# Three of a feed-forward layer's column groups by seven products of quarters: a two-layer fp32 trunk on one core

## The chip, the core and the metric

The kernel runs on one core of a Trainium2 chip. A core has five engines that run side by side, each with its own in-order queue of instructions: PE (TensorE, the matmuls; its weight loads are a second row, PEld), DVE (VectorE), ACT (ScalarE), POOL (GpSimd) and SP (SyncE, which here issues nearly all transfers). Transfers run on 16 DMA engines. Operands lie in SBUF; matmuls write into PSUM, which has eight banks of 128 x 512 fp32 values.

The metric is the device time of one execution in microseconds (us). Of before three runs are shown, and their median counts. One more execution was taken with the hardware profiler, and all durations below come from it.

## The reference

`x` has 256 tokens of width 1024, in fp32. There are two layers (`DEPTH` 2); the feed-forward width `D_FF` is 2816.

```python
def swiglu(h, w_gate, w_up, w_down):
    return (jax.nn.silu(h @ w_gate) * (h @ w_up)) @ w_down

for l in range(DEPTH):
    x = x + 0.5 * swiglu(rms_norm(x, ffn1_norm[l]), ffn1_w_gate[l], ffn1_w_up[l], ffn1_w_down[l])
    proj = rms_norm(x, mix_norm[l]) @ w_in[l]
    ...   # windowed attention out_a and differential attention out_b, from column ranges of proj
    x = x + jnp.concatenate([out_a, out_b], axis=-1) @ w_out[l]
    x = x + 0.5 * swiglu(rms_norm(x, ffn2_norm[l]), ffn2_w_gate[l], ffn2_w_up[l], ffn2_w_down[l])
return rms_norm(x, final_norm)
```

So there are four feed-forward layers (FFN 1 to 4) and two attention mixers, in the order FFN 1, mixer, FFN 2, FFN 3, mixer, FFN 4.

## The kernel before

**Three products for one.** A matmul in the type fp32r takes rounded fp32 operands. Every value v is therefore split in two: hi is v rounded to fp32r (a copy with a cast, on ACT) and lo is v - hi (a subtraction, on DVE, which writes fp32r). A product is the sum of hi x hi, lo x hi and hi x lo: three matmuls into the same PSUM bank (lines 317 to 319, `tokens`).

**The weights come in steps.** A list `specs` holds all weight loads in the order of their use; one step of the FFN is 1 MB: 4 row blocks of 128 by 512 columns. `emit_load(i)` takes the buffers `raw`, `whi` and `wlo` of step i (three of each), issues the transfer on SP's queue, and then, in two halves of 128 x 1024, the cast (ACT, line 106) and the subtraction (DVE, line 108). `weights()` hands out the operands of the step that is used now, and emits the loads of all steps up to `LOOK` = 2 ahead. A step makes 24 matmuls, since it meets both halves of the tokens (t = 0, 1).

**The FFN** (`ffn`). The hidden width is cut in column groups of 512: group 0, groups 1 to 4, and a last half group. The loop of groups 1 to 4:

```python
            hT = turn(h, 2)
            gs, us = [bank(), bank()], [bank(), bank()]
            for sl in (gs, us):
                for k0 in (0, 4):
                    tokens(sl, norm.xs, weights(), k0)
            h = hidden(gs, us)
            for hh in range(2):
                down(hT, g - 1, hh, weights())
```

Group g's gate and up columns take four steps (two row halves `k0` for each), 96 matmuls; `hidden` applies silu (ACT, line 379) and the product with up (DVE, line 384) to the four banks; and the down product of the group before it, two steps and 48 matmuls, covers that. At the head of the next group PE transposes the hidden block (8 transposes, line 398) and `split` makes its operand (lines 323 and 324). The down product adds into four banks that are held through the whole FFN.

**The operands of x.** `Norm.pair(j)` transposes two column blocks of `xk` and writes hi (ACT, line 185, from PSUM with the gain as scale) and lo (DVE, line 186). The norm's factor per token comes later, as the scale of silu and of the up product, so only these operands must be there before an FFN begins. At the end of an FFN or a mixer the residual is added (`Residual.add`, line 366), followed by the squares for the next norm (ACT, line 175); two of the four pairs are made before the last products, and two (`late`) after the next stage has begun.

**The mixers.** Eight steps of w_in and w_out there have the second half of each subtraction on POOL instead of DVE (`pooled`, line 107). The end of a mixer's head norm for the differential heads (lines 619 to 633) comes after all of the products of probabilities and values.

**The start.** SP issues the first two steps' transfers in quarters, alternating with the four transfers of x.

**Who sets the order.** Instructions are written in program order, and the framework's scheduler, which has a timeline model, may reorder them on each engine by priority; a tile pool hands a buffer out again only when its last reader is done.

Of the kernel before, what the change touches and what calls it, by code (L numbers as in the profile page):

```python
# [27 lines left out]
LOOK = 2  # L28
N_RAW, N_HI, N_LO = 3, 3, 3
N_S4 = 18  # L30
# [3 lines left out]
def trunk(ctx: ExitStack, tc: tile.TileContext, x, n1, g1, u1, d1, nm, w_in, sink,  # L34
# [29 lines left out]


    specs = []
    loaded = {}
    paired = set()
    pooled = set()
# [6 lines left out]
    def plain(w, c0, n, k0=0, kn=None):  # L76
        src = rows(w, c0, n, k0, kn)
        kn = src.shape[1]
        return (kn, n, lambda t: [(t, src)])

    def emit_load(i):
        kn, n, moves = specs[i]
        raw = wp.tile([P, kn, n], F32, tag="raw", bufs=N_RAW, name=nm_("raw"))
# [4 lines left out]
        for dst, src in moves(raw):  # L88
            if i > 1:
                sp.dma_start(dst, src)  # L90
            else:
                for a, b in zip(cuts, cuts[1:]):
                    sp.dma_start(dst[:, a:b], src[:, a:b])
                    yield
        for a, b in zip(cuts, cuts[1:]):
# [9 lines left out]
            for r_, h_, l_ in views:  # L105
                act.copy(h_, r_)  # L106
                eng = pool if i in pooled and a in cuts[2:] else dve
                eng.tensor_tensor(l_, r_, f(h_), op=ALU.subtract)  # L108
            if i < 2:
                yield  # L110
    nxt = [0, 0]

    def weights():
        i = nxt[0]
        nxt[0] += 1
        while i > 1 and nxt[1] <= min(i + LOOK, len(specs) - 1):
            for _ in emit_load(nxt[1]):
                pass
            nxt[1] += 1
        return loaded.pop(i)  # L120

    for l in range(DEPTH):
        def ffn_specs(wg, wu, wd):
# [3 lines left out]
            for g in range(1, NGRP):  # L127
                specs.extend(plain(w[l], g * 512, 512, k0, 4) for w in (wg, wu) for k0 in (0, 4))
                specs.extend(down(g - 1, h) for h in range(2))
            for k0 in (0, 4):  # L130
                def gu_moves(t, k0=k0, ws=(wg[l], wu[l])):
                    return [(t[:, :, h * 256:h * 256 + 256], rows(w, FF - 256, 256, k0, 4)) for h, w in enumerate(ws)]
                specs.append((4, 512, gu_moves))
# [10 lines left out]
        for c in range(2):  # L144
            def qa_moves(t, c=c, wi=wi):
                return [(t[:, :, h * P:(h + 1) * P], rows(wi, QA + h * 256 + c * P, P)) for h in range(2)]
            paired.add(len(specs))
            specs.append((KC, 256, qa_moves))
        for k0 in (0, 4):
            specs.append(plain(wi, VB, 512, k0, 4))  # L150
        pooled.update(range(mixed + 4, len(specs)))
# [3 lines left out]
        for k0 in (0, 2):  # L155
# [3 lines left out]
            specs.append((2, D, o_moves))  # L159
# [6 lines left out]
    class Norm:  # L166


        def __init__(self, g0):
            self.g0, self.xs = g0, []  # L170
            self.ss = tmp("nss", 2, (P, 2, 4))

        def squares(self, t, c, n):
            j_ = tmp("junk", 2, (P, 512))
            self.last = act.activation(j_[:, :n], xk[:, t, c:c + n], AF.Square, accum_out=self.ss[:, t, c // 256:c // 256 + 1])

        def pair(self, j):
            sl = halves(bank())
            for i in range(2):
                for t in range(2):  # L180
                    pe.transpose(sl[:, i, t * P:(t + 1) * P], xk[:, t, (2 * j + i) * P:(2 * j + i + 1) * P], ident)
            xs = blk()
            for i in range(2):
                g = gcol[:, self.g0 + 2 * j + i:self.g0 + 2 * j + i + 1]
                act.activation(xs[:, i, 0:S], sl[:, i], AF.Identity, scale=g)  # L185
                dve.scalar_tensor_tensor(xs[:, i, S:512], in0=sl[:, i], scalar=g, in1=f(xs[:, i, 0:S]),  # L186
                                         op0=ALU.mult, op1=ALU.subtract)
            self.xs.append(xs)
# [25 lines left out]
    early = [emit_load(0), emit_load(1)]  # L214
    for j in range(4):
        sp.dma_start(xk[:, :, j * 256:(j + 1) * 256], x[0].rearrange("(t p) d -> p t d", p=P)[:, :, j * 256:(j + 1) * 256])
        for e in early * 2 if j < 2 else ():
            next(e)
    nxt[1] = 2
# [13 lines left out]
    def take_x(k):  # L233

        if k < 2:
            for j in (2 * k, 2 * k + 1):
                norm.pair(j)
                for e in early * 2 if k == 0 else ():
                    next(e)
        else:  # L240
            for t in range(2):
                for h in range(2):
                    norm.squares(t, h * 512, 512)

    grow = const.tile([NG - 16, P], F32, name="grow")
    dist_i = const.tile([P, 512], mybir.dt.int32, name="dist_i")
# [7 lines left out]
    lin = const.tile([P, 4, DEPTH * 64], F32, name="lin")  # L254
    lsum = const.tile([P, 2, DEPTH], F32, name="lsum")
    lpr = const.tile([P, 2, DEPTH * 64], F32, name="lpr")
# [6 lines left out]
    def attention_constants():  # L263
# [6 lines left out]

        pool.iota(dist_i, pattern=[[P, 2], [-1, S]], base=0, channel_multiplier=1)
# [21 lines left out]

        for i, a in enumerate((lq1, lk1, lq2, lk2)):
            pool.dma_start(lin[:, i], a.rearrange("l d -> (l d)").partition_broadcast(P))

    def make_lam():
        for i in range(2):
# [43 lines left out]
    def first_groups(norm, ws):  # L342

        sls = [halves(bank()) for _ in ws]
        for k in range(0, KC, 2):
            if k == 4:
                norm.late()
# [12 lines left out]
    class Residual:  # L360
# [5 lines left out]
        def add(self, h, t):  # L366
            xv = xk[:, t, h * 512:(h + 1) * 512]
            dve.tensor_tensor(xv, xv, self.accs[h][t], op=ALU.add)
            self.nxt.squares(t, h * 512, 512)

        def turn(self, h):
            for j in (2 * h, 2 * h + 1):
                self.nxt.pair(j)

    def ffn(norm, aside=None, before=None, final=False):
        def gate(acc, t):
            g = tmp().rearrange("p a n -> p (a n)")
            n = acc.shape[1]
            act.activation(g[:, :n], acc, AF.Silu, scale=norm.r[:, t:t + 1])  # L379
            return g[:, :n]  # L380

        def up(h, acc, g, t):
            n = acc.shape[1]
            dve.scalar_tensor_tensor(h[:, t, :n], in0=acc, scalar=norm.hr[:, t:t + 1], in1=g, op0=ALU.mult, op1=ALU.mult)  # L384
# [7 lines left out]
        def turn(hs, n):  # L392
            out_ = []
            for i in range(n):
# [5 lines left out]
                split(hb, sl)  # L400
# [10 lines left out]
        for k0 in (0, 4):  # L411
            if before is not None:
                before(k0 // 4)
            elif k0 == 4:
                norm.late()
            ws = (weights(), weights())
            for k in (0, 2):
                for sl, w in zip((gs, us), ws):
                    tokens(sl, norm.xs, w, k0, (k, k + 1))
        if before is not None:  # L420
            before(2)
            norm.stats()
        h = hidden(gs, us)
        for g in range(1, NGRP):
            hT = turn(h, 2)
            gs, us = [bank(), bank()], [bank(), bank()]
            for sl in (gs, us):
                for k0 in (0, 4):
                    tokens(sl, norm.xs, weights(), k0)
# [3 lines left out]
            if g == 2 and aside is not None:  # L433
                with tc.issue_after(norm.last.ins):
                    aside()
# [16 lines left out]
    def ffn_close(parts, nxt):  # L452
# [11 lines left out]
        def late():  # L464
            res.turn(1)
            nxt.stats()
        nxt.late = late

    def mix(l, norm, nxt_norm):
# [15 lines left out]
        def q_finish(sl, sc):  # L485
            t = tmp()
            q = tp.tile([P, 2, 512], F32R, tag="q", bufs=3, name=nm_("q"))
            for i in range(2):
                dve.scalar_tensor_tensor(t[:, i], in0=sl[:, i], scalar=sc[i], in1=norm.R, op0=ALU.mult, op1=ALU.mult)
            split(q, t)  # L490
# [118 lines left out]
        oa = [bank() for _ in range(2)]  # L609
        for t in range(2):  # L610
            for c in range(4):
                for a in range(2):
# [6 lines left out]
        ss = tmp("ss", 1, (P, 2, HB))  # L619
        for h in range(HB):  # L620
            for t in range(2):
                j_ = tmp("junk", 2, (P, P))
                act.activation(j_, osl[t][:, h * P:(h + 1) * P], AF.Square, accum_out=ss[:, t, h:h + 1])
        d1 = den_b.rearrange("p h (t a) -> p a t h", a=2)[:, 0]
        dd = tmp("dd", 1, (P, 2, HB))
        dve.scalar_tensor_tensor(dd, in0=d1, scalar=EPS, in1=d1, op0=ALU.mult, op1=ALU.mult)
        dve.scalar_tensor_tensor(ss, in0=ss, scalar=1.0 / P, in1=dd, op0=ALU.mult, op1=ALU.add)
        rb = tmp("rb", 1, (P, 2, HB))
        pool.tensor_tensor(rb.rearrange("p t h -> p (t h)"), ss.rearrange("p t h -> p (t h)"), mhalf, op=ALU.pow)
        on = blk(F32)  # L630
        for t in range(2):
            dve.tensor_tensor(on[:, t].rearrange("p (h d) -> p h d", h=HB), osl[t].rearrange("p (h d) -> p h d", h=HB),
                              rb[:, t].unsqueeze(2).to_broadcast([P, HB, P]), op=ALU.mult)
# [18 lines left out]
        for hp, src in enumerate(turned(on)):  # L652
            dst = oT[2 + hp]
            act.activation(dst[:, :, 0:S], src, AF.Copy, scale=gsub[:, l:l + 1])
            dve.scalar_tensor_tensor(dst[:, :, S:512], in0=src, scalar=gsub[:, l:l + 1], in1=f(dst[:, :, 0:S]),
# [126 lines left out]
```

## Time and profile before

| quantity | value |
| --- | --- |
| median of three runs | 998.27 us (995.05 to 998.62) |
| the profiled execution | 997.01 us, span 995.2 us |
| mean granted PE clock in it | 0.991 of full speed |
| DMA | 169.39 MB, mean 170 GB/s, 51.3% of 16 engines' time on SP's queue |
| costliest rows, busy time | L317, L318, L319 on PE 433, 439, 437 us; L108 on DVE 375.8; L106 on ACT 323.2 |
| mean of one, 128 x 1024 | L108 1222 ns x256, L106 1050 ns |
| chain of waits, by engine | PE 90%, DVE 3%, ACT 3%, issue 2%, DMA 2% |

The rows of single matmuls overlap (their ends are modelled), so the three rows of PE add to more than its busy time; how long PE takes for one is read from the length of a stretch divided by the matmuls in it. The idle time of an engine has a releaser: what ended last of what the next instruction waited for. Idle time of an engine that doesn't set the end costs nothing. L106's idle time ends with PE's L318, that is, with the matmuls that give a `whi` buffer back: ACT and DVE prepare weights as fast as PE uses them up.

### The profile page before, as it was taken

How to read it: one execution, taken by the hardware profiler on the slowest of the kernel's cores; microseconds unless marked ns; L12 is line 12 of the kernel's file. 1: busy time of each engine (PE TensorE's matmuls, PEld its weight loads, DVE VectorE, ACT ScalarE, POOL GpSimd, SP SyncE). 2: the span in 40 equal slices, each digit the busy share in tenths (PEclk: the TensorE clock that was granted, in tenths of full speed). 3: DMA queues.
4: the chain of work that ended last, by engine and by line, in shares of the span. 5: the costliest groups of instructions: out<-in, count | busy, mean ns of one | idle time of the engine just before them, and what ended most of it. 6: DMA issues, size and time to landing. Idle time of an engine off the chain costs nothing.

```text
span 995.2 us, 12394 instructions
## 1 busy us (share of the span) xinstructions
PE 961.8 (97%) x4940; PEld 813.7 (82%) x4940; DVE 550.0 (55%) x816; ACT 476.7 (48%) x809; POOL 53.6 (5%) x78
## 2 busy tenths in 40 slices
PE   6999999999999999999999999999999999999996
PEld 5788888889798788888878888887988887888885
DVE  4645454568945555454555545456597455454553
ACT  5544443457745443434445343435477355444433
POOL 4000000004100000000000000000230000000001
PEclk9999999999999999999999999999999999999999
DMA  8655565635515555656545565555445245565531
GB/s 264 212 195 186 174 206 173 204 97 182 150 43 169 178 202 172 196 182 200 181 143 194 172 209 170 192 188 184 118 142 152 85 169 169 190 212 187 195 127 42
DMA packets 98218, 169.39 MB, mean 170 GB/s; under 512 B 3182, under 2 KB 30896, under 8 KB 98160
## 3 DMA queue, kind: packets, MB, share of 16 engines
q1 hardware_dynamic: 97872, 168.31, 51.3%
q0 software_dynamic: 288, 0.30, 0.4%
q8 instruction: 38, 0.62, 0.2%
q14 instruction: 20, 0.16, 0.0%
HBM read 167.54 MB, written 1.05 MB: 169 GB/s over the span
## 4 chain that ended last, share of the span: by engine, by line
PE 90%; DVE 3%; ACT 3%; issue 2%; DMA 2%; SPq 0%; POOLq 0%; POOL 0%; ACTq 0%; DVEq 0%
PE ps L317 25%; PE ps L318 25%; PE ps L319 25%; PE ps L398 2%; PE ps L338 2%; PE ps L339 2%; PE ps L340 2%; DMA raw<-in_ffn_w_up_dram 2%; PE ps L615 1%; DVE wlo L108 1%; ACT whi L106 1%; PE ps L567 1%; PE ps L502 1%; ACT s L512 1%; PE ps L588 1%
## 5 line engine op out<-in xcount | busy, mean ns | idle before, releaser
L108 DVE TENSOR_TENSOR wlo<-raw,whi 128x1024 fp32r<-128x1024 f32 (+2 forms) x364 | 375.8, 1076 | 338.0 <-ACT whi L106 336.1
L106 ACT CAST whi<-raw 128x1024 fp32r<-128x1024 f32 (+2 forms) x392 | 323.2, 882 | 356.0 <-PE ps L318 322.4
L317 PE MATMUL ps<-whi,s 128*128 128x512 f32 x1126 | 433.2, 393 | 6.2 <-ACT s L185 5.3
L318 PE MATMUL ps<-whi,s 128*128 128x512 f32 x1126 | 439.0, 390 | 0.0
L319 PE MATMUL ps<-wlo,s 128*128 128x512 f32 x1126 | 437.0, 390 | 0.0
L317 PEld LDWEIGHTS ps<-whi,s 128*128 128x128 f32 x1126 | 211.8, 189 | 49.7 <-ACT s L185 5.8
L318 PEld LDWEIGHTS ps<-whi,s 128*128 128x128 f32 x1126 | 212.6, 189 | 43.8 <-DVE s L186 0.5
L319 PEld LDWEIGHTS ps<-wlo,s 128*128 128x128 f32 x1126 | 212.3, 189 | 43.5
L338 PE MATMUL ps<-s,whi 128*128 128x256 f32 x224 | 64.8, 293 | 4.3 <-ACT s L185 4.3
L339 PE MATMUL ps<-s,whi 128*128 128x256 f32 x224 | 64.9, 290 | 0.0
L340 PE MATMUL ps<-s,wlo 128*128 128x256 f32 x224 | 64.4, 288 | 0.0
L379 ACT ACTIVATE tmp<-ps,r 128x512 f32<-128x512 f32 (+1 forms) x48 | 31.2, 651 | 62.9 <-PE ps L319 62.8
L384 DVE SCALAR_TENSOR_TENSOR s<-ps,hr,tmp 128x512 f32<-128x512 f32 (+1 forms) x48 | 32.7, 705 | 41.2 <-PE ps L319 24.7
L338 PEld LDWEIGHTS ps<-s,whi 128*128 128x128 f32 x224 | 43.5, 196 | 5.6 <-ACT s L185 4.8
L339 PEld LDWEIGHTS ps<-s,whi 128*128 128x128 f32 x224 | 44.3, 198 | 0.1
L340 PEld LDWEIGHTS ps<-s,wlo 128*128 128x128 f32 x224 | 44.3, 198 | 0.0
L196 POOL TENSOR_TENSOR r<-ms,mhalf 128x2 f32<-128x2 f32 x6 | 4.2, 706 | 637.7 <-DVE ms L194 637.7
L512 ACT ACTIVATE s<-s,negm 128x256 f32<-128x256 f32 x64 | 31.8, 499 | 12.4 <-DVE negm L510 12.3
L324 DVE TENSOR_TENSOR s<-ps,s 128x512 fp32r<-128x512 f32 x48 | 31.0, 684 | 8.2 <-ACT s L323 8.2
L108 POOL TENSOR_TENSOR wlo<-raw,whi 128x256 fp32r<-128x256 f32 (+1 forms) x28 | 31.7, 1156 | 62.4 <-ACT whi L106 62.4
L323 ACT CAST s<-ps 128x512 fp32r<-128x512 f32 x48 | 25.7, 583 | 12.1 <-PE ps L398 9.7
L398 PE MATMUL ps<-ident,s 128*128 128x128 f32 x176 | 24.7, 274 | 4.3 <-DVE s L384 4.3
(115 smaller groups left out, 456.4 us busy)
## 6 DMA issues: line engine op xcount, KB each, us to landing
raw<-in_ffn_w_down_dram SPq DMA_DIRECT2D x44, 1024.0 KB, 4.9
raw<-in_ffn_w_gate_dram SPq DMA_DIRECT2D x39, 1024.0 KB, 5.0
raw<-in_ffn_w_up_dram SPq DMA_DIRECT2D x39, 1024.0 KB, 5.0
raw<-in_w_in_dram SPq DMA_DIRECT2D x14, 1024.0 KB, 5.1
raw<-in_ffn_w_gate_dram SPq DMA_DIRECT2D x8, 512.0 KB, 3.7
raw<-in_ffn_w_up_dram SPq DMA_DIRECT2D x8, 512.0 KB, 4.7
raw<-in_w_in_dram SPq DMA_DIRECT2D x8, 512.0 KB, 4.6
raw<-in_w_out_dram SPq DMA_DIRECT2D x4, 1024.0 KB, 4.8
```

What stands on the lines that cost most here:

```text
L106: act.copy(h_, r_)
L108: eng.tensor_tensor(l_, r_, f(h_), op=ALU.subtract)
L317: pe.matmul(accs[t], lhsT=xh, rhs=hi[:, k], start=kk == first, stop=False)
L318: pe.matmul(accs[t], lhsT=xl, rhs=hi[:, k], start=False, stop=False)
L319: pe.matmul(accs[t], lhsT=xh, rhs=lo[:, k], start=False, stop=kk == (last if isinstance(last, int) else last[t]))
L338: pe.matmul(acc, lhsT=wh, rhs=xv[:, 0:S], start=first and i == 0 and j == 0, stop=False)
L339: pe.matmul(acc, lhsT=wh, rhs=xv[:, S:512], start=False, stop=False)
L340: pe.matmul(acc, lhsT=wl, rhs=xv[:, 0:S], start=False, stop=last and i == len(kcs) - 1 and j == 1)
L379: act.activation(g[:, :n], acc, AF.Silu, scale=norm.r[:, t:t + 1])
L384: dve.scalar_tensor_tensor(h[:, t, :n], in0=acc, scalar=norm.hr[:, t:t + 1], in1=g, op0=ALU.mult, op1=ALU.mult)
L398: pe.transpose(sl[:, c, t * P:(t + 1) * P], hs[:, t, (2 * i + c) * P:(2 * i + c + 1) * P], ident)
L512: act.activation(e[:, t, c], e[:, t, c], AF.Exp, scale=-1.0, bias=negm[:, n:n + 1], accum_out=den[:, n:n + 1])
```

## The change

In groups 1, 3 and 4 of every FFN (`SEVEN`) the four steps of gate and up are taken as a product of 2 x 2 quarters. On one side stand the quarters of x: tokens in two halves t, rows in two halves b (x00, x01, x10, x11). On the other side stand four weight quarters of 1 MB: a and d of gate (upper and lower rows), b and c of up. The eight products of a quarter by a quarter become seven (Strassen's method in Winograd's form), with sums around them: four sums of x's quarters, made once for each FFN (`make_sums`), four differences of weight quarters for each group, written in place over a raw buffer (`less`), and seven additions of 128 x 512 results for each group (`plus`). A product is now 12 matmuls, and its weight operand is used once.

Around it: six raw buffers in place of three, and transfers up to eight steps ahead, separate from the split (`AHEAD`); operands of x for an FFN go through an fp32 copy in SBUF (`operands`), since the sums need it; POOL's share of the splits goes to DVE; x is loaded on ACT's queue; group 1's transposes come after its first product (before: ahead of it); the residual's squares come after the transposes of x; the second pair of operands and the stats are spread over the next stage's first steps (`late(k)`); the head norm `norm_b` is put ahead of the last 8 of the other heads' 32 products of probabilities and values; and instructions that PE waits for get a higher priority (`urgent`).

```diff
-LOOK = 2
-N_RAW, N_HI, N_LO = 3, 3, 3
-N_S4 = 18
+LOOK, AHEAD = 2, 8
+N_RAW, N_HI, N_LO = 6, 3, 3
+N_S4 = 16
+SEVEN = (1, 3, 4)
...
+    def urgent():
+        return tc.high_priority(300)
...
+    def seven(wg, wu, c0, downs):
+        a, b, c, d = [object() for _ in range(4)]
+        def less(x, y, to):
+            def prep():
+                for h in (0, 2):
+                    x_, y_, t_ = [raws[i][:, h:h + 2] for i in (x, y, to)]
+                    dve.tensor_tensor(t_, x_, y_, op=ALU.subtract)
+            return prep
+        n = dict(kn=4, n=512, moves=None)
+        return [plain(wg, c0, 512, 0, 4, key=a, free=[]),
+                Step(4, 512, plain(wu, c0, 512, 0, 4).moves, key=b, prep=less(b, a, a), src=a, free=[]),
+                Step(4, 512, plain(wu, c0, 512, 4, 4).moves, key=c, prep=less(c, b, b), src=b),
+                Step(**n, prep=less(c, a, a), src=a, free=[]),
+                downs[0],
+                plain(wg, c0, 512, 4, 4, key=d, free=[]),
+                Step(**n, prep=less(d, a, d), src=d, free=[a, d]),
+                Step(**n, src=c),
+                downs[1]]
...
-                eng = pool if i in pooled and a in cuts[2:] else dve
-                eng.tensor_tensor(l_, r_, f(h_), op=ALU.subtract)
+                dve.tensor_tensor(l_, r_, f(h_), op=ALU.subtract)
...
+    at = dict(use=0, dma=2, prep=2, split=2)
     def weights():
-        while i > 1 and nxt[1] <= min(i + LOOK, len(specs) - 1):
-            for _ in emit_load(nxt[1]):
-                pass
-            nxt[1] += 1
+        i = at["use"]
+        at["use"] += 1
+        if i > 1:
+            while True:
+                if at["split"] <= min(i + LOOK, len(specs) - 1) and at["prep"] > at["split"]:
+                    for _ in emit_split(at["split"]):
+                        pass
+                    at["split"] += 1
+                elif at["prep"] <= min(i + LOOK + 1, len(specs) - 1) and at["dma"] > at["prep"] and \
+                        (specs[at["prep"]].prep is None or at["split"] >= at["prep"]):
+                    if specs[at["prep"]].prep is not None:
+                        specs[at["prep"]].prep()
+                    at["prep"] += 1
+                elif at["dma"] < min(i + AHEAD, len(specs)) and (specs[at["dma"]].moves is None or len(raws) < N_RAW):
...
+                    at["dma"] += 1
+                else:
+                    break
...
+        def operands(self, j, sl):
+            if self.sums:
...
+                for i in range(2):
+                    act.activation(xg[:, i], sl[:, i], AF.Identity, scale=g)
+                self.last_act = act.copy(xs[:, :, 0:S], xg)
+                self.last = dve.tensor_tensor(xs[:, :, S:512], xg, f(xs[:, :, 0:S]), op=ALU.subtract)
+                return
...
+        def make_sums(self):
+            (t0, t1), (b0, b1) = [(t[:, :, 0:P], t[:, :, P:S]) for t in self.xg]
+            def make(x, y, op):
+                v = tmp().rearrange("p a (c s) -> p (a c) s", c=2)
+                dve.tensor_tensor(v, x, y, op=op)
+                sm = blk().rearrange("p a (c s) -> p (a c) s", c=2)
+                act.copy(sm[:, :, 0:P], v)
+                dve.tensor_tensor(sm[:, :, P:S], v, f(sm[:, :, 0:P]), op=ALU.subtract)
+                self.sm.append(sm)
+                return v
+            s1 = make(t1, b1, ALU.add)
+            s2 = make(s1, t0, ALU.subtract)
+            make(t0, t1, ALU.subtract)
+            make(b0, s2, ALU.subtract)
...
-        sp.dma_start(xk[:, :, j * 256:(j + 1) * 256], x[0].rearrange("(t p) d -> p t d", p=P)[:, :, j * 256:(j + 1) * 256])
+        act.dma_start(xk[:, :, j * 256:(j + 1) * 256], x[0].rearrange("(t p) d -> p t d", p=P)[:, :, j * 256:(j + 1) * 256])
...
+        def late(self, k):
+            if k == 2:
+                self.turn(1)
+            elif k == 3:
+                self.nxt.stats()
...
+        def by_seven(h, g):
+            flat = lambda: tmp().rearrange("p a n -> p (a n)")
+            if g > 1:
+                hT = turn(h, 2)
+            acc = prod(norm.quarter(0, 0))
+            m1 = flat()
+            with urgent():
+                act.copy(m1, acc)
+            if g == 1:
+                hT = turn(h, 2)
+            m5 = prod(norm.summed(0))
+            m7 = prod(norm.summed(2))
+            m6 = prod(norm.summed(1))
+            u2 = plus(flat(), m1, m6)
+            u3 = plus(flat(), u2, m7)
+            u1 = plus(flat(), u3, m5)
+            plus(u2, u2, m5)
+            down(hT, g - 1, 0, weights())
+            acc = prod(norm.quarter(0, 1))
+            h = blk(F32)
+            g0 = plus(m1, m1, acc)
+            with urgent():
+                act.activation(g0, g0, AF.Silu, scale=norm.r[:, 0:1])
+            acc = prod(norm.quarter(1, 1))
+            g1 = plus(u3, u3, acc)
...
+            up(h, u1, g1, 1)
+            acc = prod(norm.summed(3))
+            plus(u2, u2, acc)
+            up(h, u2, g0, 0)
+            down(hT, g - 1, 1, weights())
+            return h
```

In the built program PE has 4362 instructions in the place of 4510, DVE 851 for 609, ACT 520 for 432, POOL 50 for 61, and SP 177 for 180.

More of the change, by code (lines that the diff above doesn't have):

```diff
@@ L233, in take_x @@
     def take_x(k):
[L235 to L239, printed above, removed]
-        else:
-            for t in range(2):
-                for h in range(2):
-                    norm.squares(t, h * 512, 512)
+        if k < 4:
+            norm.pair(k)
+            for e in early * 2 if k < 2 else ():
+                next(e)
+        else:
+            with tc.issue_after(norm.last_act.ins):
+                for t in range(2):
+                    for h in range(2):
+                        norm.squares(t, h * 512, 512)
+            norm.stats()
     grow = const.tile([NG - 16, P], F32, name="grow")
-    dist_i = const.tile([P, 512], mybir.dt.int32, name="dist_i")
     distB = const.tile([P, 2, S], F32, name="distB")
@@ L399, in turn @@
                 hb = blk()
[L400 removed]
+                with urgent():
+                    split(hb, sl)
                 out_.append(hb)
@@ L410, in ffn @@
         gs, us = [bank(), bank()], [bank(), bank()]
[L411 to L422, printed above, removed]
+        if before is None:
+            before = norm.late
+        before(0)
+        ws = (weights(), weights())
+        for k in (0, 2):
+            before(k // 2 + 1)
+            for sl, w in zip((gs, us), ws):
+                tokens(sl, norm.xs, w, 0, (k, k + 1))
+        before(3)
+        for sl in (gs, us):
+            tokens(sl, norm.xs, weights(), 4)
+        before(4)
         h = hidden(gs, us)
         for g in range(1, NGRP):
[L425 to L429, printed above, removed]
+            if g == 3 and aside is not None:
+                with tc.issue_after(norm.last.ins):
+                    aside()
+            if g in SEVEN:
+                h = by_seven(h, g)
+                continue
+            if g > 1:
+                hT = turn(h, 2)
+            gs = [bank(), bank()]
+            tokens(gs, norm.xs, weights(), 0)
+            if g == 1:
+                hT = turn(h, 2)
+            tokens(gs, norm.xs, weights(), 4)
+            us = [bank(), bank()]
+            for k0 in (0, 4):
+                tokens(us, norm.xs, weights(), k0)
             h = hidden(gs, us)
```

217 lines of the change are left out of this document (134 added, 83 removed).

## The prediction

> **What bounds the kernel now.** I read the page's busy shares first, then the idle gaps of PE along the timeline, then one steady column group in the view by windows and in DVE's timeline.
>
> ```profile
> PE 961.8 (97%) x4940; PEld 813.7 (82%) x4940; DVE 550.0 (55%) x816; ACT 476.7 (48%) x809; POOL 53.6 (5%) x78
> ...
> 404.22:437.75 33.53, 33.53 (x154) 27.86 (x153) 16.80 (x16) 14.15 (x17) 0.00 (x0) 1.00 0.58 188
> ...
> 371.56 2.36 DVE L108 TENSOR_TENSOR wlo<-raw,whi 128x1024 fp32r<-128x1024 f32 x2 [3.07 <-ACT whi L106]
> 373.83 1.28 DVE L324 TENSOR_TENSOR s<-ps,s 128x512 fp32r<-128x512 f32 x2
> ```
>
> The second line is one column group between two turns of the hidden block (start and length; busy time of PE, PEld, DVE, ACT, POOL; clock, DMA). PE never rests there; DVE is half idle, and its idle time ends with ACT's cast, which itself waits for PE to give a buffer back. A group has 144 matmuls (96 gate and up, 48 down) and 8 transposes (0.87 us in the chain): (33.53 - 0.87) / 144 = 0.2268 us a matmul. Its DVE work is six splits of 2.36, two hidden-block splits of 1.28 together and two up products of 1.43 together: 16.9. The third line gives DVE's rate when nothing holds it: two halves of a split take 373.83 - 371.56 = 2.27, so 1.135 each, though one alone lasts 1.222 (row L108, 302.4 us over 256).
>
> PE's real losses are few, and they lie at stage borders:
>
> ```profile
> 206.09 0.50 PE L338 MATMUL ps<-s,whi 128*128 128x256 f32 x2 [2.15 <-ACT s L185]
> 256.15 1.45 PE L502 MATMUL ps<-s,q 64*128 64x256 f32 x20 [2.02 <-DVE q L324]
> 336.86 0.44 PE L398 MATMUL ps<-ident,s 128*128 128x128 f32 x2 [1.58 <-DVE s L384]
> 502.77 1.29 PE L317 MATMUL ps<-whi,s 128*128 128x512 f32 x4 [1.96 <-ACT s L185]
> ...
> 207.00:210.00 3.00, 3.00 (x16) 3.00 (x15) 3.00 (x11) 2.36 (x7) 0.71 (x1) 0.50 0.82 231
> ...
> 311.00:314.00 3.00, 3.00 (x18) 2.55 (x17) 3.00 (x6) 2.44 (x6) 0.00 (x0) 1.00 0.06 16
> ```
>
> In brackets stands the idle time before, and its releaser. After the gap at 206 PE ran at clock 0.50 until 210. The last line is the border from the first mixer to the FFN after it: no PE idle at all.
>
> **The sum's base.** The profiled execution took 997.0 (span 995.2); the median of the runs is 1.3 above it. About 0.5% (5 us) is what a measurement here can tell from no change.
>
> **1. The products removed.** In each of twelve groups (three per FFN) seven products of 12 matmuls replace eight: 12 x 0.2268 = 2.72 a group, 32.7 in all if PE stays the bound. A new group needs 132 x 0.2268 + 0.87 = 30.8 of PE.
>
> **2. What DVE gets in those groups.** Seven weight operands, each used once, replace four used twice: nine splits a group instead of six, so 18 halves; and four quarter differences in place, 8 halves. In the trace no such difference exists; the nearest row is the split's own subtraction, same size, both inputs in SBUF: 1.135 unheld, 1.222 if each waits for the one before. I take 1.135, since in the built program's lists the two halves of a difference read data finished earlier. 26 x 1.135 = 29.5. Seven additions of 128x512 with an input in PSUM (row L324, 0.64): 4.5. With 1.28 and 1.43 as before: 36.7, against PE's 30.8 and the old period of 33.5. ACT gets 18 casts of 1.0, a copy and the rest: 21, no bound. So DVE becomes the bound inside the group, and what helps is only what it does ahead, in the half-idle group before; three hi and lo buffers and a look-ahead of two limit that.
>
> For groups 3 and 4, which follow each other, I went down the built program's queues of PE, ACT and DVE, each instruction starting when its engine, inputs and buffer are free and lasting as above. Group 2 comes out at 33.5, as measured. Groups 3 and 4 need 66.3 together: PE's 61.6, and waits of 0.8 before group 4's transposes, 1.3 at its fourth product, 0.7 at its fifth to seventh, 2.0 before the transposes after it. That last one can be checked by eye: behind the last product's bank DVE has listed an addition, two split halves, an addition, a split half and the up product, 0.64 + 2.27 + 0.64 + 1.14 + 0.7 = 5.4, while PE has 20 down matmuls, 4.5, and ACT's cast for the last half comes late. Before: 67.1. Gain 0.8 of 5.4.
>
> Group 1 of FFNs 2 to 4, from the end of group 0 to the next transposes: 34.8 (waits 0.7, 1.2, 2.2) against 33.5 + 1.58: gain 0.3. So 1.1 an FFN for the three: -3.3; groups 3 and 4 of the first FFN: -0.8.
>
> **3. The entries of FFNs 2 to 4.** Before, ACT writes the rounded operand from PSUM directly (L185, 0.46) and PE starts. Now it writes both halves in plain fp32 to SBUF and then casts them (0.55), with other casts listed between. After the mixer's last matmul ACT's list holds a square (0.62), two operand passes (0.84), two weight casts that wait for the buffer PE has just left (2.0), then the cast: 4.0 before PE's first matmul. The border at 311 cost nothing. At the third FFN: two casts 2.0, square 0.63, four passes 1.7, square 0.63, cast 0.55: 5.5, against 1.96 above. Sum: 4.0 + 3.5 + 4.0 = +11.5. These waits are not in the trace; between zero (if the list lets PE cover them) and this, I take the list.
>
> **4. The clock.** A gap near 2 us brought half clock for 3.4 us (1.7 us lost) at 206, 502 and 694, and not at 255 nor at 336 (1.58). Two entries newly get a gap of 4: +3.4. Six gaps near 2 (four behind group 4, two behind group 1) at half odds: 6 x 0.5 x 1.7 = +5, bounds 0 and 10. The Trainium skill (TensorE: Matmul & The Clock Gate, in the table on what matters for kernels) warns only of gaps above about 3 us; by it the six would cost nothing and the sum would be 5 lower. The trace has half clock after 1.96 and 2.15, so the trace decides.
>
> **5. The start.** x comes on ACT's queue, loads 2 and 3 no longer wait for a raw buffer: at the 259 GB/s of the first 26 us, 5 MB are in by about 22, and group 0 ends near 33 instead of 38. But the first up product stands on DVE behind the difference c - b; c is the eighth MB (2.2 + 8 x 1.05 MB / 0.26 = 34), so the transposes start near 40 as before (39.7), only with 12 matmuls done; and DVE's debt, 6.4 of waiting before group 2, takes that back and 1.9 more. Bounds -5 and +6. One half-clock stretch goes, one comes.
>
> **6. The mixers.** POOL's split halves go to DVE. They cost DVE time already:
>
> ```profile
> 242.52 3.34 DVE L108 TENSOR_TENSOR wlo<-raw,whi 128x512 fp32r<-128x512 f32 x2
> ...
> 242.31 2.99 POOL L108 TENSOR_TENSOR wlo<-raw,whi 128x512 fp32r<-128x512 f32 x2 [5.29 <-ACT whi L106]
> ```
>
> Two that alone take 1.28 took 3.34 beside POOL; four on DVE alone are 2.56. So -1 a mixer (the gap at 255 stands behind the second such pair), and -0.5 for the head norm put between the last products (gap at 288, 0.45): -3. Bounds -6 and +6. The Trainium skill (SBUF, Who interferes with whom) says that a vector instruction with two SBUF inputs and a GpSimd instruction that reads SBUF lock each other out; the trace agrees here. One who counted POOL's work as free help would have added 7 a mixer instead.
>
> **Sum.** -3.3 - 0.8 + 11.5 + 3.4 + 5 + 1.9 - 3 = +14.7; a third of the differences held (1.222) adds 96 x 0.087 / 3 = 2.8. 997.0 + 17.5 = 1014.5.
>
> **The rivals.**
> *PE stays the bound.* DVE runs far enough ahead, groups fall to 30.8, entries are covered as at 311: 997 - 33 = 964; half of it, 981. For: DVE is at 55% and the order was rebuilt with priorities for what PE waits for. Against: 36.7 over 30.8, and only two steps of lead. 0.20, of which 0.07 for the full gain.
> *A draw.* The entries are hidden, the rest stands: 1014.5 - 15 = 1000. 0.10.
> *Every DVE instruction held.* All 26 at 1.222: 12 x 26 x 0.087 = 27 more than 1.135, so 1039; it decides once DVE waits on itself in each chain, for the additions too. The Trainium skill (VectorE: DVE Perf Modes, on the drain) says that the next instruction does not start before the pipe is empty, and that one that isn't held starts earlier; the 2.27 of the pair supports the second half. 0.10.
> *Loads late.* Two of six raw buffers (a and c) are held through most of a group; if SP's in-order queue, where each load waits for a buffer, falls behind by one landing (4.9) in each of the twelve: +59, 1070. Against: DMA is at 58% in a group, and loads are listed several steps ahead. 0.05, and 0.05 for part of it.
> *The forecast*, DVE-bound groups without gain and longer entries: 0.50, alone within 1003 to 1028.
>
> The range 984 to 1036 leaves out the full gain and the upper ends of the last two. Faster 0.20, same 0.10, slower 0.70.
>
> **What would show it.** Right: DVE over 95% busy in groups 3 and 4, near 66 for the pair; PE idle released by DVE before transposes; gaps of 4 to 5.5 released by ACT at three entries; more stretches at clock 0.5. Wrong: periods near 31, PE idle under 1% in them (steps 2 and 3 fall); differences at 1.22 start to start (the drain); PE waiting for raw (the loads).

## The result, and the profile after

The changed kernel took 1000.5 us (median of 12 runs, 998.35 to 1001.19) against 997.35 of the kernel before in the same series: 1.0029 times as long, 95% interval 1.0019 to 1.0038. That is 0.3% slower, inside what the prediction called no change; it had forecast 1014.5. The profiled execution took 999.4, span 997.4.

The page's busy shares and, below them, its chain by engine:

```profile
PE 938.8 (94%) x4796; PEld 788.0 (79%) x4796; DVE 799.9 (80%) x1112; ACT 577.7 (58%) x927; POOL 25.7 (3%) x50
...
PE 77%; DVE 15%; ACT 4%; issue 2%; DMA 1%; POOL 0%; POOLq 0%; DVEq 0%; ACTq 0%
```

PE has 144 instructions and 23 us less, DVE 250 us more, and DVE stands in the chain with 15% in place of 3%. FFN 2 by windows, from the end of group 0: group 1, 2, 3, 4 (columns as before):

```profile
339.47:372.35 32.88, 31.00 (x141) 25.38 (x139) 32.88 (x36) 22.92 (x25) 0.00 (x0) 1.00 0.64 218
372.35:405.96 33.61, 33.61 (x152) 27.93 (x153) 21.76 (x21) 12.26 (x14) 0.00 (x0) 1.00 0.48 162
405.96:437.61 31.65, 30.97 (x141) 25.47 (x139) 31.26 (x34) 20.55 (x23) 0.00 (x0) 1.00 0.58 200
437.61:472.05 34.44, 31.91 (x140) 25.30 (x141) 34.44 (x36) 21.97 (x25) 0.00 (x0) 1.00 0.56 187
```

DVE never rests in groups 1 and 4. Group 2 (eight products) is as long as before, and DVE has 5 us more in it than its own 16.8: that is the work it does ahead for group 3. PE's timeline, the waits that matter:

```profile
73.34 0.69 PE L574 MATMUL ps<-ident,s 128*128 128x128 f32 x2 [6.08 <-DVE s L509]
314.21 2.07 PE L431 MATMUL ps<-whi,s 128*128 128x512 f32 x4 [3.65 <-ACT s L263]
372.35 1.09 PE L574 MATMUL ps<-ident,s 128*128 128x128 f32 x8 [1.88 <-DVE s L509]
472.05 0.44 PE L574 MATMUL ps<-ident,s 128*128 128x128 f32 x2 [1.53 <-DVE s L509]
505.99 2.08 PE L431 MATMUL ps<-whi,s 128*128 128x512 f32 x4 [4.17 <-ACT s L263]
```

Two kinds: an FFN's first matmul waits for ACT's cast of the operand (L263; 802.87 has a third, 3.64), and transposes wait for DVE's up product (L509). ACT's timeline at 311 shows the detour with the weight casts inside it:

```profile
310.92 0.84 ACT L262 ACTIVATE s<-ps,gcol 128x256 f32<-128x256 f32 x2
311.63 2.00 ACT L147 CAST whi<-raw 128x1024 fp32r<-128x1024 f32 x2
313.52 0.64 ACT L263 CAST s<-s 128x512 fp32r<-128x512 f32 x1
```

### The profile page after: what moved, and what is told of

Read it like the earlier page. It is cut to its first block, busy times and chain, and to the rows that moved or that the text cites. A ratio compares the mean times of both kernels' runs of the same rounds, so it can differ in the third digit from the quotient of the medians.

```text
span 997.4 us, 12586 instructions
## 1 busy us (share of the span) xinstructions
PE 938.8 (94%) x4796; PEld 788.0 (79%) x4796; DVE 799.9 (80%) x1112; ACT 577.7 (58%) x927; POOL 25.7 (3%) x50
## 4 chain that ended last, share of the span: by engine, by line
PE 77%; DVE 15%; ACT 4%; issue 2%; DMA 1%; POOL 0%; POOLq 0%; DVEq 0%; ACTq 0%
PE ps L431 15%; PE ps L432 15%; PE ps L433 15%; DVE wlo L148 8%; PE ps L516 5%; PE ps L518 5%; PE ps L517 5%; DVE raw L104 4%; PE ps L452 3%; PE ps L453 3%; PE ps L454 3%; DVE tmp L527 2%; ACT whi L147 2%; PE ps L574 2%; PE ps L832 1%
## 5 line engine op out<-in xcount | busy, mean ns | idle before, releaser
L147 ACT CAST whi<-raw 128x1024 fp32r<-128x1024 f32 (+2 forms) x464 | 396.3, 909 | 288.0 <-PE ps L432 112.0
L148 DVE TENSOR_TENSOR wlo<-raw,whi 128x1024 fp32r<-128x1024 f32 (+2 forms) x464 | 462.9, 1042 | 114.1 <-ACT whi L147 113.2
L431 PE MATMUL ps<-whi,s 128*128 128x512 f32 x742 | 286.4, 396 | 14.2 <-ACT s L263 13.3
L432 PE MATMUL ps<-whi,s 128*128 128x512 f32 x742 | 290.8, 392 | 0.0
L433 PE MATMUL ps<-wlo,s 128*128 128x512 f32 x742 | 283.7, 392 | 0.0
L431 PEld LDWEIGHTS ps<-whi,s 128*128 128x128 f32 x742 | 141.0, 191 | 44.8 <-ACT s L263 14.8
L433 PEld LDWEIGHTS ps<-wlo,s 128*128 128x128 f32 x742 | 140.6, 190 | 30.1 <-DVE wlo L148 1.7
L432 PEld LDWEIGHTS ps<-whi,s 128*128 128x128 f32 x742 | 141.2, 190 | 28.4
L516 PE MATMUL ps<-whi,s 128*128 128x512 f32 x336 | 132.7, 395 | 3.4 <-ACT whi L147 3.4
L517 PE MATMUL ps<-whi,s 128*128 128x512 f32 x336 | 130.9, 389 | 0.0
L518 PE MATMUL ps<-wlo,s 128*128 128x512 f32 x336 | 129.2, 392 | 0.3 <-DVE wlo L148 0.2
L104 DVE TENSOR_TENSOR raw<-raw,raw 128x1024 f32<-128x1024 f32 x96 | 113.8, 1216 | 0.0
L516 PEld LDWEIGHTS ps<-whi,s 128*128 128x128 f32 x336 | 63.1, 188 | 17.5 <-ACT whi L147 5.2
L518 PEld LDWEIGHTS ps<-wlo,s 128*128 128x128 f32 x336 | 63.1, 188 | 15.5 <-DVE wlo L148 2.4
L517 PEld LDWEIGHTS ps<-whi,s 128*128 128x128 f32 x336 | 63.1, 188 | 12.5
L527 DVE TENSOR_TENSOR tmp<-tmp,ps 128x512 f32<-128x512 f32 x84 | 55.8, 678 | 0.0
L452 PEld LDWEIGHTS ps<-s,whi 128*128 128x128 f32 x224 | 42.8, 194 | 5.4 <-ACT s L268 4.8
```

What stands on the lines that cost most here:

```text
L104: dve.tensor_tensor(t_, x_, y_, op=ALU.subtract)
L148: dve.tensor_tensor(l_, r_, f(h_), op=ALU.subtract)
L431: pe.matmul(accs[t], lhsT=xh, rhs=hi[:, k], start=kk == first, stop=False)
L432: pe.matmul(accs[t], lhsT=xl, rhs=hi[:, k], start=False, stop=False)
L433: pe.matmul(accs[t], lhsT=xh, rhs=lo[:, k], start=False, stop=kk == (last if isinstance(last, int) else last[t]))
L452: pe.matmul(acc, lhsT=wh, rhs=xv[:, 0:S], start=first and i == 0 and j == 0, stop=False)
```

## The experiments

Theory 1: the groups by seven are bound by DVE, and the operands' detour through fp32 makes the entries longer. Rivals: PE is the bound and something else in the change loses the time; or the entries' waits come from the new order.

**e1_direct: operands written from PSUM, the fp32 copy behind them**

```diff
-  act.activation(xg[:, i], sl[:, i], ...); act.copy(xs[:, :, 0:S], xg); dve lo from xg
+  act.activation(xs[:, i, 0:S], sl[:, i], ...); dve lo from sl      # as before
+  act.activation(xg[:, i], sl[:, i], ...)                           # copies(), behind them
```

> The changed kernel, but the operands of x at an FFN's entry are written as before (hi by ACT straight from PSUM, lo by DVE from PSUM), and the fp32 copy for the sums is a further ACT pass behind them. Theory 1 (the detour through fp32, with the casts listed inside it, makes the three entry gaps of 3.65, 4.17 and 3.64 us and the longer half-clock stretches): the gaps go back to about 0, 2 and 0, so -9.5, and -3 to -4 of half clock: 985 to 989. Rival (the gaps come from the new order around the entry, that is, squares and casts ahead of any operand pass): gaps stay over 3, time within 997 to 1001.

Measured 999.07, 1.0018 (1.0009 to 1.0028) of before. The time is near the rival's and far from theory 1's 985 to 989; the gaps are theory 1's: at the entries they did go (0, 1.97 and 0), so the detour makes them. But most of the time came back elsewhere, before transposes that wait for DVE; PE's timeline:

```profile
46.08 0.66 PE L574 MATMUL ps<-ident,s 128*128 128x128 f32 x2 [10.84 <-DVE s L509]
371.59 0.44 PE L574 MATMUL ps<-ident,s 128*128 128x128 f32 x2 [1.57 <-DVE s L509]
562.84 0.69 PE L574 MATMUL ps<-ident,s 128*128 128x128 f32 x2 [5.50 <-DVE s L509]
```

In FFN 3 the distance from the last half group before it (471.37) to these transposes is 91.5, and 91.3 in the changed kernel: nothing won. Group 1 of FFN 2 now takes 36.0 where it took 32.9, and DVE is busy for 35.9 of it. While PE waited at the entry, DVE was working ahead for group 1; without that wait PE comes earlier and waits there instead. FFNs 2 and 4 still win 3.3 and 2.4 from the mixer's first matmul to group 2's transposes, but the start loses 2.6 (a wait of 10.84 where it was 6.08), and half clock behind FFN 3's gap of 5.50 loses 2.0.

**e2_eight (eight products everywhere, sums and detour kept) and e3_eight_nosums (neither)**

```diff
-SEVEN = (1, 3, 4)
+SEVEN = ()
@@ e3_eight_nosums, in addition
-        def __init__(self, g0, sums=True):
+        def __init__(self, g0, sums=False):
```

> The changed kernel with eight products in all groups (SEVEN empty); the operands by the fp32 detour and the sums of x are kept, though nothing reads the sums. Theory 1 (the seven products are bound by DVE and earn little: groups 3 and 4 come to 66.1 where eight would take 67.1, group 1 to 32.9 where eight would take 33.5 to 35, and FFN 1 loses 5 by them): without them +4 +3 -5, 1000 to 1004, DVE near 55 to 60% busy. Rival (PE is the bound and the products earn their 2.7 a group, and the rest of the change loses it): about 1030.

> As the run with eight products in all groups, and in addition no sums and no fp32 detour: what is left of the change is the order of work, the six raw buffers, x on ACT's queue and the splits of POOL on DVE. Theory 1: the entry gaps go (9.5, and 3 of half clock), so 12 less than that run, 988 to 991, that is, 7 to 10 less than before: the mixers give 2 x 2, the start 3 to 5, group 1 the rest. Rival (the rest of the change is worth nothing by itself): 996 to 999.

Measured 997.91 (1.0001; 0.9989 to 1.0013) and 980.37 (0.982; 0.9802 to 0.9838). The first lies below the 1000 to 1004 expected: as they stand the products lose some 2.6 (1000.5 against 997.9), and the rival's gain of 30 is not there. The rest of the change is worth 17 us, more than the 7 to 10 expected: from the transposes of one last half group to the next, 166.9 against 174.3 in FFN 1, 292.8 against 296.9 and 292.8 against 296.8 over the two mixers. Sums and detour cost 17.5; the prediction had given the entries 11.5 and their half clock 3.4.

**e4_nodiff: the weight differences left out**

```diff
-                    dve.tensor_tensor(t_, x_, y_, op=ALU.subtract)
+                    pass
```

> The changed kernel without the four differences of weight quarters of each group (96 DVE instructions of 128 x 1024 are left out, so the output differs). Theory 1 (DVE is the bound inside the groups): 26 halves become 18, 36.4 us of DVE a group become 27.3, under PE's 30.8; groups 3 and 4 fall from 66.1 to 62 to 63, group 1 by 1.9, and the gap of 6.1 in FFN 1 goes with its half clock: 972 to 980. Rival (waits on banks, casts or the order in the queues set the groups): 995 to 1000.

Measured 966.0, 0.9678 (0.9656 to 0.9701): better than expected. Groups 3 and 4 of FFN 2 by windows:

```profile
388.53:419.35 30.82, 30.82 (x141) 25.60 (x140) 27.59 (x29) 20.69 (x23) 0.00 (x0) 1.00 0.61 205
419.35:450.17 30.82, 30.82 (x142) 25.61 (x141) 27.59 (x29) 20.74 (x23) 0.00 (x0) 1.00 0.71 237
```

With DVE at 27.6 (27.3 expected), PE does not wait and a group takes 30.8, as worked out. Against e2_eight the products now earn 31.9 (twelve times 2.72 is 32.7), and the differences cost 34.5. So theory 1 holds for the groups, and the sum of the change reads: rest -17.1, sums and detour +17.5, products -31.9, differences +34.5; together +3.0. These are steps taken in one order, and they don't hold in another: in the changed kernel itself the detour is worth only 1.4 (e1_direct), because DVE's lateness then shows in its place.

Theory 2 follows: a group by seven is worth having where DVE has a half-idle group ahead of it and a free one behind. Its rival: the sums and copies cost PE time wherever the groups stand.

**f1_direct_two_four (groups 2 and 4 by seven, direct operands) and f2_direct_eight (none by seven, the sums kept, direct operands)**

```diff
-SEVEN = (1, 3, 4)
+SEVENS = [(2, 4), (2, 4), (2, 4), (2, 4)]   # f1_direct_two_four: one entry an FFN
+SEVEN = ()                                  # f2_direct_eight
```

> The changed kernel with direct operands (as in e1_direct) and only groups 2 and 4 of every FFN by seven products. Theory 2 (a group by seven products needs 36.4 us of DVE against 30.8 of PE, and DVE gets about 5 us ahead in a half-idle group before it; so a group that stands alone takes about 31.5, and one that follows the sums or another such group pays a wait): each of the eight groups gains about 2 on 33.5, from the 980.4 of e3_eight_nosums, 962 to 970. Rival (the sums and copies at the entry cost DVE and ACT time that PE waits for wherever the groups stand): 974 to 984, no better than eight products without sums.

> Eight products in all groups, the sums of x still made (nothing reads them), operands direct. Between e2_eight (997.9) and e3_eight_nosums (980.4) lie 17.5: theory 2 says that the fp32 detour before the first matmul makes nearly all of it, and that the work of the sums is hidden: 980 to 984. Rival (the sums' 12 DVE and 4 ACT passes and the copies cost it): 988 to 996.

Measured 966.04 (0.969; 0.9677 to 0.9702) and 980.08 (0.9821; 0.9807 to 0.9836). Both as theory 2 has it: the sums themselves are free, the detour alone is the 17.5 of the eight products (in the two profiles 9.5 at the three entries, 1.8 before FFN 1's first matmul, 6.3 of half clock), and eight groups gain 14. What is left in f1_direct_two_four is one wait behind each group:

```profile
387.13 1.09 PE L578 MATMUL ps<-ident,s 128*128 128x128 f32 x8 [0.69 <-DVE s L513]
```

**f3_no_pool and f4_x_act: two parts of the rest, each alone in the kernel before**

```diff
-        pooled.update(range(mixed + 4, len(specs)))          # f3_no_pool
-        sp.dma_start(xk[:, :, j * 256:(j + 1) * 256], ...)   # f4_x_act
+        act.dma_start(xk[:, :, j * 256:(j + 1) * 256], ...)
```

> The kernel before with POOL's split halves on DVE, nothing else changed. Theory: two halves took 3.3 on DVE beside POOL and 1.3 alone, and the gap of 2.0 at 256 and 743 stands behind such a pair; without POOL the gap goes: -2 a mixer, 992 to 994. Rival (DVE, now with four halves, is as late): 996 to 999.

> The kernel before with the four loads of x on ACT's queue, nothing else changed (three raw buffers, two steps ahead). Theory (the start's gap of 3.4 at 26 with its half clock of 1.7 comes from x behind the weights on SP's queue): 991 to 994. Rival (the start's gain of 7.6 in e3_eight_nosums comes from the six raw buffers and the order of group 0, not from the queue): 996 to 999.

Measured 991.21 (0.9945; 0.9932 to 0.9958) and 990.77 (0.9944; 0.9932 to 0.9956): -5.3 and -5.7 of the 17; if these two add, 6 are left that were not taken apart. Both lie just below what theory expected. In f3_no_pool the two gaps of 2.0 are gone. In f4_x_act the gap of 3.4 at 26 is gone, and group 1's transposes start at 33.9 in place of 39.7.

**g1_look3, g2_look3_134, g3_direct_one_three: a longer look-ahead, and another place**

```diff
-LOOK, AHEAD = 2, 8          # g1_look3: groups 2 and 4; g2_look3_134: groups 1, 3 and 4
-N_RAW, N_HI, N_LO = 6, 3, 3
-N_S4 = 16
+LOOK, AHEAD = 3, 8
+N_RAW, N_HI, N_LO = 5, 4, 4
+N_S4 = 14
@@ g3_direct_one_three (LOOK 2): FFN 1, then FFNs 2 to 4
+SEVENS = [(3,), (1, 3), (1, 3), (1, 3)]
```

> As f1_direct_two_four, with splits three steps ahead in place of two: four hi and four lo buffers, five raw buffers, and 14 in place of 16 blocks of 4 KB a partition to make room. Theory 2 (what DVE gets ahead before a group by seven products is limited by the buffers): DVE starts a group about 3 us further ahead, and the wait of 0.69 before the transposes behind each of the eight groups goes, with what else keeps the period at 31.7 over 30.8: 957 to 961. Rival (the wait stands behind the last product whatever the lead, since DVE's list there is in program order, or the fewer blocks and raw buffers cost it): 964 to 970.

> The changed kernel (groups 1, 3 and 4) with direct operands and the deeper look-ahead of g1_look3. Theory 2: 12 groups of 36.4 on DVE; with 3 us more lead for group 1 and for the pair 3 and 4, some 6 an FFN less waiting than in e1_direct (999.1), and the 10.8 and 5.5 gaps there shrink: 972 to 984, still behind two groups an FFN. Rival (the look-ahead is not what limits DVE): 995 to 1000.

> Direct operands and look-ahead of two as in f1_direct_two_four, but groups 1 and 3 (in the first FFN group 3 alone) in place of 2 and 4. Theory 2: group 3 gains 2 as group 4 did; group 1 stands right behind the sums of x and loses its gain to waits (2.8 and 5.5 us of them in e1_direct): 971 to 978. Rival (where the groups stand is of no weight): seven groups of 2 from 980, 965 to 968.

Measured 956.0 (0.9587; 0.9574 to 0.96), the best of all; 1021.13 (1.024; 1.0226 to 1.0254), a clear miss; and 978.03 (0.981; 0.9797 to 0.9824), the upper end of what was expected. In g1_look3 PE no longer waits for DVE in groups 2 and 4; the first of them in FFN 2:

```profile
352.20:383.03 30.83, 30.83 (x141) 25.61 (x140) 28.55 (x30) 20.56 (x23) 0.00 (x0) 1.00 0.70 242
```

The eight periods, 30.8 in place of 31.7, are 6.7 of the 10 us won over f1_direct_two_four. Another 3.4 in the two profiles are half clock, which follows two of three gaps near 2 us there and none here; the last section shows why that is chance.

In g2_look3_134 PE waits 8.43 before group 2's transposes in FFN 2. DVE's timeline there:

```profile
367.88 1.27 DVE L527 TENSOR_TENSOR tmp<-tmp,ps 128x512 f32<-128x512 f32 x2
369.07 4.62 DVE L148 TENSOR_TENSOR wlo<-raw,whi 128x1024 fp32r<-128x1024 f32 x4
373.61 0.68 DVE L527 TENSOR_TENSOR tmp<-tmp,ps 128x512 f32<-128x512 f32 x1
374.21 1.21 DVE L148 TENSOR_TENSOR wlo<-raw,whi 128x1024 fp32r<-128x1024 f32 x1
375.35 0.67 DVE L527 TENSOR_TENSOR tmp<-tmp,ps 128x512 f32<-128x512 f32 x1
375.94 2.35 DVE L148 TENSOR_TENSOR wlo<-raw,whi 128x1024 fp32r<-128x1024 f32 x2
378.21 1.40 DVE L509 SCALAR_TENSOR_TENSOR s<-tmp,hr,tmp 128x512 f32<-128x512 f32 x2
381.44 0.69 DVE L438 TENSOR_TENSOR s<-ps,s 128x512 fp32r<-128x512 f32 x1 [1.82 <-ACT s L437]
```

PE has finished all its matmuls at 371.2, and seven split halves, all for later steps, stand between DVE's additions and the up product that PE needs. Behind that up product DVE rests for 1.82.

**h1_look23_134, i1_buffers, i2_look3_one_three: what made g2_look3_134 slow**

```diff
+        def prod(xo):                     # h1_look23_134
+            hi, lo = weights(2)           # a product by seven asks for splits two steps ahead
@@ i1_buffers: e1_direct with
+N_RAW, N_HI, N_LO = 5, 3, 3
+N_S4 = 14
@@ i2_look3_one_three: g1_look3 with
+SEVENS = [(3,), (1, 3), (1, 3), (1, 3)]
```

> As g2_look3_134 (1021.1), but a product of a group by seven asks for splits only two steps ahead; all other steps ask for three. Theory 3 (with three steps the halves for later steps stand in DVE's list between the last product's addition and the up product, so PE runs dry in front of the transposes; DVE's total is the same): the waits of 4.8 to 8.4 before the transposes fall to 1 to 3, as in e1_direct, and their half clock goes: 985 to 996. Rival (the order of the list has no weight, five raw buffers or 14 blocks make g2_look3_134 slow): 1012 to 1022.

> As e1_direct (groups 1, 3 and 4, direct operands, two steps ahead), with only the smaller numbers of g2_look3_134: five raw buffers and 14 blocks, three hi and lo buffers. If the buffers' numbers make g2_look3_134 slow: 1012 to 1022. If the third step of look-ahead does (DVE runs splits ahead of the additions and up products): 996 to 1004, near the 999.1 of e1_direct.

> As g1_look3 (three steps ahead), with groups 1 and 3 (group 3 alone in the first FFN) in place of 2 and 4. If group 1, behind the sums, is the place that the deeper look-ahead makes worse (its wait was 8.4 in g2_look3_134 against 1.6 in e1_direct): three such waits with their half clock, less a gain of 0.9 in each group 3: 985 to 1000, slower than the 978.0 with two steps. If only the pair 3 and 4 is: 958 to 966.

Measured 1020.81 (1.0242; 1.0228 to 1.0256), 998.22 (1.0008; 0.9997 to 1.002) and 980.88 (0.983; 0.9815 to 0.9846). The first is a miss, and the third lies in neither of its two ranges. The smaller numbers of buffers cost nothing, so the third step of look-ahead, with its fourth hi and lo buffers, is what is left. h1_look23_134 tests less than it was meant to: in its trace the same seven halves stand between the same additions at 369 to 378, so the edit did not change that list, and by this run theory 3 is neither shown nor refuted.

The traces of g2_look3_134 and i1_buffers say more. In group 1 of FFN 2, from DVE's first addition to the transposes, 19.3 us pass with three steps and 15.2 with two, and DVE rests in neither. Three more split halves (12 against 9) and one more up product stand in between: 3 x 1.135 + 0.67 = 4.1. The wait is 6.9 longer (8.43 against 1.53), by these 4.1 and by 2.8 that PE comes to it earlier. So what DVE's list holds ahead of the up product accounts for the longer wait, as theory 3 has it; a run that changes this order alone is missing.

In i2_look3_one_three group 1 behind a mixer waits 8.44 in FFNs 2 and 4, yet only 0.46 in FFN 3, where 20 halves of splits and differences stand between group 0's last up product and group 1's first, and not 26; group 3 waits nowhere. So the third step hurts where DVE comes late (group 1 behind a mixer, and the pair 3 and 4, with 4.80 in place of 1.53 behind FFN 2's) and helps groups that stand alone.

## Why the prediction was wrong

The mechanism was right: DVE is the bound in the groups, the entries wait for ACT's cast, the rest gains a little. The sum was too large by 15, and three of its terms make nearly all of that: group 1, half clock, and the differences held. Its terms against the trace of the changed kernel, span against span (997.4 - 995.2 = +2.2):

| term | predicted | measured |
| --- | --- | --- |
| groups 3 and 4, four FFNs | -3.2 | -3.2 (66.1 a pair against 66.3 forecast; FFN 1 66.9) |
| group 1, FFNs 2 to 4 | -0.9 | -6.7 (32.9, 32.4, 32.9 against 34.8 forecast; before 35.4, 34.1, 35.4) |
| entries | +11.5 | +9.5 (3.65 + 4.17 + 3.64 - 1.96) |
| half clock | +8.4 | +3.2 |
| start, to group 3's transposes of FFN 1 | +1.9 | +1.9 (108.99 - 107.11) |
| mixers | -3 | -4.1 |
| a third of the differences held | +2.8 | 0 |
| the rest: last half groups, groups 2, the end | 0 | +1.5 |

Half clock is what is lost behind the gaps by windows of 2 us, the start left out: 8.3 against 5.1. The mixers' figure is what remains from a mixer's first matmul to the end of the next group 0 (131.6 against 129.0 and 132.3 against 129.0) without the gaps of 3.65 and 3.64 and the half clock that these stretches have more than before (0.93, 1.67): -2.0 and -2.1.

**Step 2, group 1 (6 us).** The walk down the queues began at the end of group 0 as if PE had come there without a wait, and step 3 then put the wait at the entry in front. The two lie in series, and DVE works during the first: the wait at the entry pays for most of group 1's. e1_direct, which has no wait at the entries of FFNs 2 and 4, shows group 1 of FFN 2 at 36.0, above the 34.8. The same lateness was counted twice. A slip in the base is small beside it: 33.5 + 1.58 was taken for all three, but before, group 1's transposes of FFN 3 wait 0.30, not 1.58.

**Step 3, the entries (2 us).** The list was the right choice, and its lengths were a little too great: 3.65 and 3.64 for 4.0, and 4.17 at the third FFN for 5.5.

**Step 4, the short gaps (5 us).** Half odds were given to six gaps "near 2". The gaps that came were 1.37 to 1.88, and none of them brought half clock; the last section shows that such gaps are too short for it. There the figure of the Trainium skill (TensorE: Matmul & The Clock Gate, the table on what matters for kernels), by which they cost nothing, was the better one; the 1.96 and 2.15 of the trace of before were taken as the same kind of gap and are not. The gap of 2.16 before 207.85 cost nothing by luck; the same place had lost 1.7 before.

**The sum's last term (2.8 us).** No difference was held. DVE's timeline in group 4, two differences and what follows:

```profile
454.58 2.35 DVE L104 TENSOR_TENSOR raw<-raw,raw 128x1024 f32<-128x1024 f32 x2
456.85 0.68 DVE L527 TENSOR_TENSOR tmp<-tmp,ps 128x512 f32<-128x512 f32 x1
```

456.85 - 454.58 = 2.27, so 1.135 each, the rate that step 2 had taken from the splits of before. The mean length of one is 1216 ns, but the next begins before it ends. An addition takes 0.60 from start to start in this trace, where step 2 had 0.64, so a group needs 36.4 of DVE and not 36.7.

**The rivals.** The draw came true, but not by its own mechanism: the entries were not hidden. "PE stays the bound" fell in this kernel and holds in the groups 2 and 4 of g1_look3; half of its gain, 981, had lain outside the range as well, though the prediction says this of the full gain alone. The loads were not late: ACT's casts wait for a transfer twice, 1.2 us in all, in the view of waits (5.0 before). Where a term was right, it was still a sum of gains and losses that the forecast had not seen apart: 17 us gained by the rest of the change were below the surface, since DVE's debt and the detour took them back.

## What to carry to other kernels

Fewer matmuls pay only if the engine that prepares their operands has the time: add up that engine's work for the new group (here 36.4 on DVE against 30.8 on PE), and place such groups where a lighter one stands before and behind them (966 with two groups an FFN, 999 with three, both with direct operands). Waits in series that go back to one late engine are not added: whoever takes away the first finds it at the second. And a change that moves little should be taken apart: here a gain of 17 us was to be had without its main idea, and 41 with two thirds of it, operands written directly and one more step of look-ahead.

## What the runs showed of the hardware

PE's idle time and its clock: over all sixteen profiled executions (gaps of over 1.2 us, the start left out; clock in the stretch from 1 to 3 us after PE resumed), none of the 38 gaps of 1.37 to 1.88 us was followed by a clock under 0.9, 26 of the 49 of 1.96 to 2.17 were, and 31 of the 32 of 3.03 to 10.85. Two gaps of the same length in the changed kernel, 2.16 before 207.85 and 2.16 before 695.02, by windows behind them:

```profile
208.00:211.00 3.00, 3.00 (x26) 3.00 (x27) 2.89 (x11) 2.59 (x8) 0.72 (x1) 1.00 0.61 169
695.02:698.00 2.98, 2.98 (x14) 2.98 (x15) 2.47 (x9) 2.56 (x8) 0.70 (x1) 0.50 0.51 143
```

The clock is 1.00 behind the one and 0.50 behind the other. So at about 2 us the length alone does not decide.

The place does. In each trace the stretches of half clock begin whole multiples of 3.413 us apart (before: 25.86, 206.77, 503.73 and 694.88, which lie 53, 87 and 56 such steps apart), and but for the one at the very end they last one to four steps. If this grid is carried through the whole trace, 2.10 of the 2.16 us before 695.02 lie within one step; of those before 207.85, 1.16 lie in one step and 1.00 in the next. Over all 119 gaps, the 57 with at least 1.904 us in one step were followed by half clock. The 62 with at most 1.902 were not, the one of 3.63 among them: it stands before 301.35 in e4_nodiff, cut into 1.90 and 1.73. The grid lies differently in the sixteen executions, so whether a gap near 2 us costs 1.7 more is chance; none of the gaps of up to 1.88 did.

The Trainium skill's warning of gaps above about 3 us (same page and table) agrees with the 31 of 32 and leaves out the 26.
